# Values' products stored in two unsummed halves for ten of seventeen row tiles, and GpSimd's rotation issued behind VectorE's scalings

## The chip, the cores and the metric

The kernel runs on one core of one Trainium2 chip. Its five engines are TensorE (PE in the profile; PEld are its weight loads), VectorE (DVE), ScalarE (ACT), GpSimd (POOL) and SyncE (SP), which issues the DMAs. Each engine works through its own queue in order and waits there for what other engines and DMAs have to deliver. The metric is the device time of one execution in microseconds (us).

## The reference

One layer of a hybrid decoder: sliding-window attention (A) and gated linear attention (B) side by side, one output projection over both, then a squared-ReLU MLP, for 2048 prompt positions and 8 x 8 sample positions, with D = 1024. Cut to what the change touches (normalisations, the branch B and the MLP are left out):

```python
q = rope(q); k = rope(k)                       # 8 query heads, 2 key heads, 64 wide
s = einsum(q, k) * 64**-0.5                    # 128 queries against 256 keys, banded
m = maximum(max(s), sink)
p = exp(s - m);  p = p / (sum(p) + exp(sink - m))
attn = einsum(p, v)                            # 512 columns
mix = concat([attn, gla_out]) @ w_out          # 512 + 512 columns -> 1024
x = x + rms_norm(mix)
```

## The kernel before, in words

**Stages.** The rows are cut in 16 tiles of 128 prompt rows and one of 64 sample rows (NTILE = 17, NB = 16). Attention runs from about 30 to 305 us of the profiled span, the gated linear attention to about 735, the output projection to about 911, the MLP to the end.

**Precision.** Float32 products are made of parts: an operand is copied to a rounded high half by ScalarE, and VectorE forms the low half as the difference (`split_copy`, L226, does both: ScalarE in L228, VectorE in L229). A product takes high by high, high by low and low by high.

**Attention.** The loop `for i in range(NB)` (L794) takes a row tile in an iteration, with four `unit`s (L458), each for one key head r and two of its query heads (jj). A unit goes: scores (PE, tile `sc`), mask and maximum (DVE, a custom instruction that writes `s` and `m`), exponential (ACT, with the sum into `den`), reciprocal of `den` and two scalings of `s` by it (DVE, TENSOR_SCALAR), transposes `pT` (PE), the halves `ph` (ACT) and `pl` (DVE), the product `av` (PE). The values `vv` hold high and low half side by side, 64 columns each, so that `av` has two halves of 64 partitions, which must be summed: ACT copies the upper half to `rest`, and DVE adds it to the lower one into `mo` (64 partitions x 256). When the four units of a tile are done, one DMA stores `mo` to DRAM (`mix_d`), through `stores` and `store` (L326).

Three units are under way at a time (`behind`, `now`, `ahead`). What belongs to coming tiles is put between them: the table `A_PLAN` (L58) says at which unit (0 to 3) and which phase (A, X, B, C) the step `do` (L821) issues a piece: `x_norm` (L316, name "junk"), the projections' results (`take_first`, `take_rest`, L350 and L356), the halves of x (`x0`, `x1`), the low halves of queries and keys (`lo0`, `lo1`) and the rotation ("turn", `rotate`, L378). Between them PE gets projection matmuls (`proj`) as filling (`A_FILL`). The wrappers `te`, `ac` and `dv` hold the order of the program on PE, ACT and DVE (all under the line of the helper, L141). GpSimd and SyncE have no such wrapper: a scheduler places their instructions by what is ready.

**GpSimd in an iteration:** the rotation of a coming tile (two products `tb` with the sines, L385; the product `qk` with the cosines, L391; two sums into `rot`, L394 and L400), casts that copy keys to the other 64 partitions (L432 to L443), the sinks' columns of `s` (L466), and in eight of the iterations two subtractions for the weights of the next stage (`split_gw`, L273).

**Output projection.** `load_mix` (L1299) loads a tile's 1024 columns with one DMA (L1311) and splits them; `out_projecting` (L1324) makes two halves of 512 output columns with 24 matmuls each, over k = 0 to 7 blocks of 128 mix columns (L1337; 0 to 3 are attention's, 4 to 7 the other branch's). `residual` (L1507) normalises, adds and prepares the MLP's input; its powers run on GpSimd (L218). The order of the tiles is 0, 4, 1, 5, 2, 6, 3, 7, sample, 8, 12, 9, 13, 10, 14, 11, 15.

Of the kernel before, what the change touches and what calls it, by code (L numbers as in the profile page):

```python
# [21 lines left out]
P = 128  # L22
# [35 lines left out]
A_PLAN = [(name, (int(at[0]), at[1])) for name, at in dict(  # L58
    first="1B", hi1="3B", x1="1B", lo1="0A", x0="0C", rest="3A", lo0="3A", junk="2A", turn="1A", rstd="1A", vl="3B"
).items()]  # L60
G_FIRST = (0, 1)
G_NEXT = (NB, *range(2, NB))
G_ORDER = (3, 0, 1, 2)
G_FILL, G_GM = (38, 14, 13), 9
G_LAST = 32
G_HELD = 5
S_WAIT = (2, 3, 6)
WO_PARTS = ((), (0, 1, 2), (3, 4, 5), (6, 7))
# [58 lines left out]
def f32(ap):  # L127
    return ap.bitcast(F32)
# [23 lines left out]
def hybrid_step_kernel(ctx: ExitStack, tc: tile.TileContext, I, O):  # L152
# [12 lines left out]
    def rows(i):  # L165
        return min(P, NTOK - i * P)
# [25 lines left out]
    dpool = ctx.enter_context(tc.tile_pool(name="dpool", bufs=1, space=DRAM))  # L192
    mix_d = [dpool.tile([P, KT, rows(i)], F32, name=f"mix_d{i}") for i in range(NTILE)]
    xt_d = [dpool.tile([P, 2, KT, rows(i)], F32, name=f"xt_d{i}") for i in range(NTILE)]
    h_d = [dpool.tile([P, 7, KT // 2, BT], F32, name=f"h_d{sb}") for sb in range(NSB)]
# [90 lines left out]
    gxTs, ropes, xs_in, xTs, proj, qks, rots, heads, vals = {}, {}, {}, {}, {}, {}, {}, {}, {}  # L286
    stores = []

# [37 lines left out]
    def store():  # L326

        for dst, src in stores:
            nc.sync.dma_start(dst, src)
        stores.clear()  # L330

    def project(i, c, kind="a", wide=0):
# [23 lines left out]
    def take_rest(i):  # L356

        n = rows(i)
        p_ = proj.pop((i, 1))
        w = 640 - A_N  # L360
        scaled(qks[i].rearrange("p h d -> p (h d)")[:n, A_N:640], i, p_[:n, :w])
        vps = p_[:n, w:A_N]
        if i == NB:
            vals[i] = vn = sp.tile([NS, P], F32, tag="vv", name="vn", bufs=4)
            scaled(vn, i, vps)
            return lambda: None
        vals[i] = vv = sp.tile([P, 2, 2, HD], F32R, tag="vv", name=f"vv_{i}", bufs=4)
        vh, vl = vv[:, :, 0, :], vv[:, :, 1, :]
        vps = vps.rearrange("p (r d) -> p r d", r=2)
        scaled(vh, i, vps)  # L370
        if i == NB - 1:
            vo = sp.tile([P, P], F32, tag="kc", name="vo", bufs=1)
            scaled(vo, i, p_[:n, w:A_N])
            stores.append((O["v_win_prompt"][0, 0].rearrange("w h d -> w (h d)"), vo))
        rs = rstd_all[:n, i : i + 1]
        return lambda: dv.scalar_tensor_tensor(vl, vps, rs, f32(vh), op0=ALU.mult, op1=ALU.subtract)

    def rotate(i, engine=nc.gpsimd):  # L378
# [78 lines left out]

    def unit(i, r, jj, mo):  # L458

# [30 lines left out]
        for u in range(2):  # L490
            dv.tensor_scalar(s[:, u, :nk], s[:, u, :nk], den[:, u : u + 1], None, op0=ALU.mult)
        yield
        pT = bank([P, nkt, 2, P], "c", f"pT_{u_}")
# [14 lines left out]
        both = [v.rearrange("p u d -> p (u d)") for v in both]  # L508
        out = mo[rr, jj * 2 : jj * 2 + 2].rearrange("p j q -> p (j q)")
        if nkt == 1:  # L510
            te.matmul(av[:HD], hi[0], ph[:, 0], start=True, stop=False)
            te.matmul(av[:HD], hi[0], pl[:, 0], start=False, stop=False)
            te.matmul(av[:HD], lo[0], ph[:, 0], start=False, stop=True)
            yield
            ac.activation(out, av[:HD], AF.Copy)
        else:
            te.matmul(av, both[0], ph[:, 0], start=True, stop=False)
            for kt in range(2):
                te.matmul(av[:HD], hi[kt], pl[:, kt], start=False, stop=False)
            te.matmul(av, both[1], ph[:, 1], start=False, stop=True)  # L520
            yield
            rest = sp.tile([P, 2 * P], F32, tag="spc", name=f"rest_{u_}", bufs=2)
            ac.activation(rest[:HD], av[HD:], AF.Copy)
            yield
            dv.tensor_tensor(out, av[:HD], rest[:HD], op=ALU.add)
        if (r, jj) == (1, 1):
            stores.append((mix_d[i][:, 0:4, :], mo))
        yield

    def sample_unit(c, r, cached, kcs, mo):  # L530
# [39 lines left out]
        yield  # L570
        pc = sp.tile([P, 2, P], F32, tag="spc", name=f"spc_{r}_{c}", bufs=2)
        dv.tensor_copy(pc[:, 0, :], pt[:, 0, :])
# [206 lines left out]
    def units():  # L779
        for i in range(NB):  # L780
            mo = sp.tile([P, 4, P], F32, tag="mo", name=f"mo_{i}", bufs=2)
            for u in range(4):
                yield unit(i, u // 2, u % 2, mo)
# [10 lines left out]
    for i in range(NB):  # L794
# [18 lines left out]
        new = i + 3 < NTILE  # L813
        todo["turn"] = lambda: run(rotate(i + 1))
        if i + 2 < NTILE:
            todo["first"] = lambda: take_first(i + 2)
            todo["rest"] = lambda: todo.update(vl=take_rest(i + 2))
        if new:
# [6 lines left out]

        for u in range(4):
            for unit_ in (behind, now) if u in A_PL_FIRST else (now, behind):
                next(unit_, None)
# [33 lines left out]
    fill = chain(fill, *(projecting(t, gxTs[t], G_LATE, ac) for t in G_FIRST))  # L862
    for n in range(4):
        later = next(queue, None)
        next(now)
# [426 lines left out]
    def first_mixes():  # L1292
        ln, lh = logs[NB - 1]
        for i in B_ORDER[:2]:
            with tc.issue_after(ln.ins), tc.issue_after(lh.ins):
                deque(load_mix(i), 0)
            yield

    def load_mix(i, lo=None, hi=None):  # L1299
        n = rows(i)  # L1300
# [9 lines left out]
        ks = KT // 2 if i == NB - 1 else KT  # L1310
        nc.sync.dma_start(f32(m[:, 0, :ks, :n]), mix_d[i][:, :ks])  # L1311
        yield
        if i == NB:
            split_copy(m[:, 1, :, :NS], m[:, 1, :, NS:], f32(m[:, 0, :, :NS]))
            mixes[i] = m[:, 1], None
            return
        split_copy(m[:, 1, :ks, :n], m[:, 2, :ks, :n], f32(m[:, 0, :ks, :n]))
        parts = [[m[:, u, k, :n] for k in range(ks)] for u in (1, 2)]
# [5 lines left out]
    def out_projecting(te, i, banks, kinds="aabb"):  # L1324
# [3 lines left out]
        for c in range(2):  # L1328
            p_ = next_bank(kinds, f"out_{i}_{c}")
            cc = slice(c * 512, (c + 1) * 512)  # L1330
            for k in range(KT):
                if i == NB:
                    products = [(mh[:, k], w) for w in wo[k]]
                else:
                    products = (mh[k], wo[k][0]), (mh[k], wo[k][1]), (ml[k], wo[k][0])
                for u, (x, w) in enumerate(products):
                    te.matmul(p_, x, w[:, cc], start=k + u == 0, stop=k == KT - 1 and u == len(products) - 1)  # L1337
                    yield
            banks.append(p_)
# [96 lines left out]
    turned, logs, seconds = {}, {}, []  # L1436
    early = []
    fill = products()
# [35 lines left out]
    for p in H_EARLY:  # L1474
        h_place(0, p)
    U, R = {}, {}
    open_pools(U, ("raw", "xs", "ah", "al", "bh", "bl", "st1", "t"), "u")
# [753 lines left out]
```

## Time and profile before

| what | value |
|---|---|
| median of three runs | 2219.06 us (2218.36 to 2219.94) |
| the profiled execution's own time | 2217.48 us |
| its span, first to last instruction | 2215.7 us |
| ACT busy in the span | 1222.5 us (55%) |
| POOL busy in the span | 250.6 us (11%) |
| PE's granted clock, mean of the span | 0.999 |

The profiler's times are counted from the span's first instruction; 1.8 us of the execution lie outside it. A line of a timeline is: start in us, duration in us, engine, source line, operation, output<-input by the program's names, and the shape; "x2" are two instructions shown as one, and a bracket at the end tells how long the engine sat idle before it and what ended that. A group line holds a count, then the least, median and greatest duration in ns, and the first and last start. A window's line holds its bounds and length, then the busy time of PE, PEld, DVE, ACT and POOL, the mean granted clock, the DMA share and GB/s.

### The profile page before, as it was taken

How to read it: one execution, taken by the hardware profiler on the slowest of the kernel's cores; microseconds unless marked ns; L12 is line 12 of the kernel's file. 1: busy time of each engine (PE TensorE's matmuls, PEld its weight loads, DVE VectorE, ACT ScalarE, POOL GpSimd, SP SyncE). 2: the span in 40 equal slices, each digit the busy share in tenths (PEclk: the TensorE clock that was granted, in tenths of full speed). 3: DMA queues.
4: the chain of work that ended last, by engine and by line, in shares of the span. 5: the costliest groups of instructions: out<-in, count | busy, mean ns of one | idle time of the engine just before them, and what ended most of it. 6: DMA issues, size and time to landing. Idle time of an engine off the chain costs nothing.

```text
span 2215.7 us, 34304 instructions
## 1 busy us (share of the span) xinstructions
PE 2177.0 (98%) x11947; PEld 1865.5 (84%) x11947; DVE 1580.2 (71%) x3221; ACT 1222.5 (55%) x2549; POOL 250.6 (11%) x408
## 2 busy tenths in 40 slices
PE   8999999999999999999999999999999999999998
PEld 8888888899999888888888888888888888888886
DVE  5888877777778776687667788878545545855557
ACT  6777766555566443555555655555444444554445
POOL 3466522111111110000000000000000000000000
PEclk9999999999999999999999999999999999999999
DMA  7343322121113455765555766766765755866665
GB/s 240 120 139 138 108 95 89 57 73 62 53 49 120 157 192 195 261 224 185 200 189 189 273 208 212 242 233 221 230 207 178 232 175 184 292 232 217 219 196 202
DMA packets 229798, 392.64 MB, mean 177 GB/s; under 512 B 23379, under 2 KB 137882, under 8 KB 225642
## 3 DMA queue, kind: packets, MB, share of 16 engines
q1 hardware_dynamic: 229626, 390.47, 52.3%
q8 instruction: 94, 1.54, 0.3%
q14 instruction: 78, 0.64, 0.1%
HBM read 255.54 MB, written 135.86 MB: 177 GB/s over the span
## 4 chain that ended last, share of the span: by engine, by line
PE 83%; DVE 10%; ACT 5%; issue 2%; DMA 1%; POOL 0%; SPq 0%; DVEq 0%; ACTq 0%; POOLq 0%
PE dn L141 27%; PE gproj L141 10%; PE uc L141 7%; PE ua L141 7%; PE out L1337 6%; PE ud L141 4%; PE ub L141 4%; PE ue L141 4%; DVE s L141 2%; PE out L141 2%; PE sam L141 1%; PE proj L141 1%; PE gm L141 1%; PE dsam L141 1%; DVE pl L141 1%
## 5 line engine op out<-in xcount | busy, mean ns | idle before, releaser
L141 PE MATMUL dn<-ot,os 128*128 128x512 f32 x2688 | 621.2, 389 | 0.6 <-DVE ot L141 0.4
L141 PEld LDWEIGHTS dn<-ot,os 128*128 128x128 f32 x2688 | 504.2, 188 | 107.1 <-DVE ot L141 2.0
L141 DVE TENSOR_TENSOR os<-os 128x512 fp32r<-128x512 f32 x224 | 154.7, 690 | 228.1 <-ACT os L141 228.0
L141 ACT ACTIVATE os<-os 128x512 fp32r<-128x512 f32 x224 | 141.4, 631 | 278.1 <-DMA os<-s_d 219.5
L141 PE MATMUL gproj<-wg,gx 128*128 128x384 f32 (+1 forms) x1408 | 269.0, 343 | 0.0
L141 PEld LDWEIGHTS gproj<-wg,gx 128*128 128x128 f32 x1408 | 244.1, 188 | 5.0 <-issue 3.3
L141 ACT ACTIVATE st<-st 128x512 f32<-128x512 f32 x225 | 142.3, 633 | 137.4 <-DVE st L141 132.2
L141 PE MATMUL ua<-H,w 128*128 128x512 f32 x744 | 179.7, 390 | 0.3 <-DVE w L141 0.3
L141 PE MATMUL uc<-H,s 128*128 128x512 f32 x744 | 179.0, 389 | 0.0
L141 PEld LDWEIGHTS uc<-H,s 128*128 128x128 f32 x744 | 139.4, 188 | 29.2 <-DVE st L141 0.4
L141 PEld LDWEIGHTS ua<-H,w 128*128 128x128 f32 x744 | 138.5, 188 | 29.2 <-DVE w L141 1.1
L218 POOL TENSOR_TENSOR frs<-rs_v,half 128x1 f32<-128x1 f32 (+1 forms) x13 | 9.8, 751 | 1222.6 <-DVE rs_v L141 1222.6
L141 DVE TENSOR_TENSOR st<-st 128x512 f32<-128x512 f32 x160 | 110.4, 692 | 48.6 <-ACT st L141 45.4
L1337 PE MATMUL out<-wo,mt 128*128 128x512 f32 x608 | 141.5, 391 | 0.0
L1337 PEld LDWEIGHTS out<-wo,mt 128*128 128x128 f32 x608 | 113.2, 188 | 23.0
L141 ACT ACTIVATE s<-t 128x1024 fp32r<-128x1024 f32 x62 | 65.7, 1059 | 62.7 <-PE ue L141 24.6
L141 DVE TENSOR_TENSOR s<-t,s 128x1024 fp32r<-128x1024 f32 x62 | 75.9, 1225 | 33.9 <-ACT s L141 31.0
L141 DVE TENSOR_TENSOR ot<-ot 128x512 fp32r<-128x512 f32 x128 | 88.2, 689 | 10.9 <-ACT ot L141 9.8
L141 PE MATMUL proj<-wa_hi,xh 128*128 128x384 f32 (+1 forms) x272 | 95.2, 353 | 0.9 <-ACT wa_hi L141 0.6
L141 PE MATMUL proj<-wa_lo,xh 128*128 128x384 f32 (+1 forms) x272 | 93.9, 349 | 0.0
L141 PE MATMUL proj<-wa_hi,xl 128*128 128x384 f32 (+1 forms) x272 | 92.7, 345 | 0.0
L141 ACT ACTIVATE ot<-ot 128x512 fp32r<-128x512 f32 x128 | 80.8, 631 | 17.5 <-DMA ot<-t_d 13.5
(424 smaller groups left out, 4053.2 us busy)
## 6 DMA issues: line engine op xcount, KB each, us to landing
os<-s_d SPq DMA_DIRECT2D x224, 256.0 KB, 2.8
s_d<-st SPq DMA_DIRECT2D x31, 1792.0 KB, 8.9
raw<-in_w_up SPq DMA_DIRECT2D x64, 512.0 KB, 6.8
ot<-t_d SPq DMA_DIRECT2D x128, 256.0 KB, 3.2
rt<-in_w_down SPq DMA_DIRECT2D x96, 256.0 KB, 3.0
t<-in_w_down SPq DMA_DIRECT2D x64, 256.0 KB, 3.3
t_d<-t SPq DMA_DIRECT2D x32, 512.0 KB, 7.0
gx<-xt_d SPq DMA_DIRECT2D x28, 512.0 KB, 5.3
```

The lines of the kernel that those rows point to most:

```text
L141: ins = call(*a, **k)
L218: nc.gpsimd.tensor_tensor(out, v[:n], e, op=ALU.pow)
L1337: te.matmul(p_, x, w[:, cc], start=k + u == 0, stop=k == KT - 1 and u == len(products) - 1)
```

## The change

**1. Sums left out in ten tiles.** `FOLDED` names the tiles that keep the sum (0, 1, 4, 11, 14, 15, 16). In the others ACT copies all 128 partitions of `av` to a tile of its own (`mq`), and DVE adds nothing; the halves go to DRAM apart, the lower to `mix_d`, the upper to a new `low_d`. Stores are now issued unit by unit at the start of the next one (`store_folds`), 64 x 256 each: 4 for a tile that keeps its sum, 8 for one that doesn't, 104 for the 16 prompt tiles in place of 16.

**2. The sum is made later.** `load_mix` loads `low_d` too, into a single buffer `low` (the first, of tile 5, into another place), GpSimd adds the attention half of the loaded tile to it (128 x 512), and the split runs in two halves of 512 columns, the other branch's first.

**3. The order of k.** The output projection takes the blocks 4 to 7 first, then 0 to 3.

**4. The rotation.** That of tile i+2 is issued in iteration i at 3C (`tb`, `tb`, `qk`) and in iteration i+1 at 0C (`rot`, `rot`), each behind a GpSimd memset of the `den` of the unit scaled last, which has to wait for VectorE's scalings. Tile 1's stays as it was.

```diff
+    first="1B", ..., turn="1A", rstd="1A", vl="3B", begin="3C", turned="0C"
+K_ORDER = (4, 5, 6, 7, 0, 1, 2, 3)
+FOLDED = (0, 1, 4, 11, 14, 15, 16)
...
+    def store_folds():
+        for dst, src in folds:
+            nc.sync.dma_start(dst, src)
+        folds.clear()
...
+    def behind_scaling():
+        if not scaled_by:
+            return nullcontext()
+        return tc.issue_after(nc.gpsimd.memset(scaled_by[-1], 0.0).ins)
...
         for u in range(2):
             dv.tensor_scalar(s[:, u, :nk], s[:, u, :nk], den[:, u : u + 1], None, op0=ALU.mult)
+        scaled_by.append(den)
...
-            rest = sp.tile([P, 2 * P], F32, tag="spc", name=f"rest_{u_}", bufs=2)
-            ac.activation(rest[:HD], av[HD:], AF.Copy)
-            yield
-            dv.tensor_tensor(out, av[:HD], rest[:HD], op=ALU.add)
-        if (r, jj) == (1, 1):
-            stores.append((mix_d[i][:, 0:4, :], mo))
+            if i in FOLDED:
+                rest = sp.tile([P, 2 * P], F32, tag="spc", name=f"rest_{u_}", bufs=1)
+                ac.activation(rest[:HD], av[HD:], AF.Copy)
+                yield
+                dv.tensor_tensor(out[:HD].rearrange("p j q -> p (j q)"), av[:HD], rest[:HD], op=ALU.add)
+            else:
+                ac.activation(out.rearrange("p j q -> p (j q)"), av, AF.Copy)
+                yield
+        for half, to in zip(half_of, (mix_d, low_d)):
+            if to is mix_d or i not in FOLDED:
+                folds.append((to[i][rr, jj * 2 : jj * 2 + 2, :], out[half]))
...
-        todo["turn"] = lambda: run(rotate(i + 1))
+        if i == 0:
+            todo["turn"] = lambda: run(rotate(1))
+        def begin_turn(turn):
+            with behind_scaling():
+                run(turn, 2)
+            todo["turned"] = lambda: end_turn(turn)
+        def end_turn(turn):
+            with behind_scaling():
+                run(turn)
...
+            todo["begin"] = lambda: begin_turn(rotate(i + 2))
...
+        if i not in FOLDED:
+            low = fold_place()
+            nc.sync.dma_start(low, low_d[i])
...
+            nc.gpsimd.tensor_tensor(low, low, raw[:, :4], op=ALU.add)
+            split_copy(m[:, 1, 4:], m[:, 2, 4:], raw[:, 4:])
+            split_copy(m[:, 1, :4], m[:, 2, :4], low)
```

**Three places in the order of instructions.** The first is GpSimd's queue between iterations 6 and 7, where tile 8 is rotated; `kl` are the keys' casts, `s` the sinks' columns, `wg` the weights of the next stage. Before:

```order
L443 CAST kl_7_2230<-kl_7_2230 64x128
L385 TENSOR_TENSOR tb_8_2393<-qk_8_2182,rope_8_1506 128x10x32 x2
L391 TENSOR_TENSOR qk_8_2182<-qk_8_2182,rope_8_1506 128x640
L394 TENSOR_TENSOR rot_8_2397<-qk_8_2182,tb_8_2393 128x2x4x64
L400 TENSOR_TENSOR rot_8_2397<-qk_8_2182,tb_8_2393 128x128
L466 COPY s_7_1_0_2327<-sink_401 128x2
L443 CAST kl_7_2230<-kl_7_2230 64x128
L437 CAST kl_8_2492<-kl_7_2230 128x2x128
L466 COPY s_7_1_1_2403<-sink_401 128x2
L273 TENSOR_TENSOR wg3_1_190<-wg3_raw6_2116,wg3_0_189 128x400
```

and with the change:

```order
L458 CAST kl_7_2282<-kl_7_2282 64x128
L391 MEMSET den_6_1_1_2312 128x2
L400 TENSOR_TENSOR tb_8_2363<-qk_8_2233,rope_8_1547 128x10x32 x2
L406 TENSOR_TENSOR qk_8_2233<-qk_8_2233,rope_8_1547 128x640
L481 COPY s_7_1_0_2385<-sink_417 128x2
L458 CAST kl_7_2282<-kl_7_2282 64x128
L452 CAST kl_8_2548<-kl_7_2282 128x2x128
L391 MEMSET den_7_0_0_2379 128x2
L409 TENSOR_TENSOR rot_8_2444<-qk_8_2233,tb_8_2363 128x2x4x64
L415 TENSOR_TENSOR rot_8_2444<-qk_8_2233,tb_8_2363 128x128
L481 COPY s_7_1_1_2459<-sink_417 128x2
L276 TENSOR_TENSOR wg3_1_206<-wg3_raw6_2169,wg3_0_205 128x400
```

The products now stand behind a memset of unit (6,1,1)'s sums, and the sums `rot` have moved behind the casts and behind a second memset, of unit (7,0,0)'s.

The second is VectorE's queue at the scalings of unit (7,1,1), a tile that no longer sums; `vv` are values, the ISA rows the masks of the next unit. Before:

```order
L141 RECIPROCAL den_7_1_1_2521<-den_7_1_1_2521 128x2
L141 TENSOR_SCALAR s_7_1_1_2403<-s_7_1_1_2403,den_7_1_1_2521 128x256 x2
L141 TENSOR_TENSOR mo_7_2199<-av_7_1_0_2544,rest_7_1_0_2549 64x256
L141 SCALAR_TENSOR_TENSOR vv_9_2525<-proj_9_1_2339,rstd_all_175,vv_9_2525 128x2x64
L855 COPY c_864_1520<-c_raw1_1512 64x8
L141 ISA s_8_0_0_2462,m_8_0_0_2579<-sc_8_0_0_2556,amask_206,sink_401 128x256
```

and with the change:

```order
L143 RECIPROCAL den_7_1_1_2578<-den_7_1_1_2578 128x2
L143 TENSOR_SCALAR s_7_1_1_2459<-s_7_1_1_2459,den_7_1_1_2578 128x256 x2
L143 SCALAR_TENSOR_TENSOR vv_9_2582<-proj_9_1_2397,rstd_all_191,vv_9_2582 128x2x64
L889 COPY c_864_1560<-c_raw1_1552 64x8
L143 ISA s_8_0_0_2518,m_8_0_0_2641<-sc_8_0_0_2612,amask_222,sink_417 128x256
```

The sum `mo` is gone; everything else stands as it stood.

The third is GpSimd's queue in the output projection, where before there are only the powers of `residual`; with the change:

```order
L221 TENSOR_TENSOR ssq1_199<-rs_v_9661,half_189 128x1
L1364 TENSOR_TENSOR mo0_5048<-mo0_5048,mt_5_9664 128x512
L1364 TENSOR_TENSOR low_9897<-low_9897,mt_2_9895 128x512
L221 TENSOR_TENSOR ssq0_198<-rs_v_9798,half_189 128x1
L221 TENSOR_TENSOR ssq1_199<-rs_v_9874,half_189 128x1
L221 TENSOR_TENSOR ssq0_198<-rs_v_9960,half_189 128x1
L1364 TENSOR_TENSOR low_9991<-low_9991,mt_6_9989 128x512
```

The late sums (L1364) of tiles 5, 2 and 6 stand among the powers, those of tiles 5 and 2 ahead of a power of tile 0.

More of the change, by code (lines that the diff above doesn't have):

```diff
@@ L58 @@
 A_PLAN = [(name, (int(at[0]), at[1])) for name, at in dict(
-    first="1B", hi1="3B", x1="1B", lo1="0A", x0="0C", rest="3A", lo0="3A", junk="2A", turn="1A", rstd="1A", vl="3B"
+    first="1B", hi1="3B", x1="1B", lo1="0A", x0="0C", rest="3A", lo0="3A", junk="2A", turn="1A", rstd="1A", vl="3B", begin="3C", turned="0C"
 ).items()]
 G_FIRST = (0, 1)
+K_ORDER = (4, 5, 6, 7, 0, 1, 2, 3)
 G_NEXT = (NB, *range(2, NB))
@@ L193, in hybrid_step_kernel @@
     mix_d = [dpool.tile([P, KT, rows(i)], F32, name=f"mix_d{i}") for i in range(NTILE)]
+    low_d = [dpool.tile([P, 4, P], F32, name=f"low_d{i}") for i in range(NB)]
     xt_d = [dpool.tile([P, 2, KT, rows(i)], F32, name=f"xt_d{i}") for i in range(NTILE)]
@@ L286, in hybrid_step_kernel @@
     gxTs, ropes, xs_in, xTs, proj, qks, rots, heads, vals = {}, {}, {}, {}, {}, {}, {}, {}, {}
-    stores = []
+    stores, folds, scaled_by = [], [], []
     stages = [("cache_k", 1), ("cache_v", 1), ("s", 3), ("ph", 2), ("pl", 2), ("qh", 2), ("ql", 2), ("mo", 2), ("tb", 1)]
@@ L456, in heads_T, with unit @@
         }
-    def unit(i, r, jj, mo):
+    def unit(i, r, jj):
         nkt = min(i + 1, 2)
@@ L508, in unit @@
         both = [v.rearrange("p u d -> p (u d)") for v in both]
-        out = mo[rr, jj * 2 : jj * 2 + 2].rearrange("p j q -> p (j q)")
+        out = sp.tile([P, 2, P], F32, tag="mq", name=f"mq_{u_}", bufs=4)
         if nkt == 1:
+            assert i in FOLDED
             te.matmul(av[:HD], hi[0], ph[:, 0], start=True, stop=False)
@@ L514, in unit @@
             yield
-            ac.activation(out, av[:HD], AF.Copy)
+            ac.activation(out[:HD].rearrange("p j q -> p (j q)"), av[:HD], AF.Copy)
         else:
@@ L570, in sample_unit @@
         yield
-        pc = sp.tile([P, 2, P], F32, tag="spc", name=f"spc_{r}_{c}", bufs=2)
+        pc = sp.tile([P, 2, P], F32, tag="mq", name=f"spc_{r}_{c}", bufs=4)
         dv.tensor_copy(pc[:, 0, :], pt[:, 0, :])
@@ L780, in units @@
         for i in range(NB):
-            mo = sp.tile([P, 4, P], F32, tag="mo", name=f"mo_{i}", bufs=2)
             for u in range(4):
-                yield unit(i, u // 2, u % 2, mo)
+                yield unit(i, u // 2, u % 2)
         mo = sp.tile([P, 4, NS], F32, tag="mo", name="mo_s", bufs=2)
@@ L826, in hybrid_step_kernel @@
         for u in range(4):
+            store_folds()
             for unit_ in (behind, now) if u in A_PL_FIRST else (now, behind):
@@ L863, in hybrid_step_kernel @@
     for n in range(4):
+        store_folds()
         later = next(queue, None)
@@ L1297, in first_mixes, with fold_place @@
             yield
+    def fold_place():
+        if not R:
+            return next(mos)
+        return R["x"].tile([P, 4, P], F32, tag="low", name="low", bufs=1)
     def load_mix(i, lo=None, hi=None):
@@ L1316, in load_mix @@
             return
-        split_copy(m[:, 1, :ks, :n], m[:, 2, :ks, :n], f32(m[:, 0, :ks, :n]))
+        raw = f32(m[:, 0])
+        if i in FOLDED:
+            split_copy(m[:, 1, :ks, :n], m[:, 2, :ks, :n], raw[:, :ks, :n])
+        else:
+            nc.gpsimd.tensor_tensor(low, low, raw[:, :4], op=ALU.add)
+            split_copy(m[:, 1, 4:], m[:, 2, 4:], raw[:, 4:])
+            split_copy(m[:, 1, :4], m[:, 2, :4], low)
         parts = [[m[:, u, k, :n] for k in range(ks)] for u in (1, 2)]
@@ L1330, in out_projecting @@
             cc = slice(c * 512, (c + 1) * 512)
-            for k in range(KT):
+            for n, k in enumerate(K_ORDER):
                 if i == NB:
@@ L1336, in out_projecting @@
                 for u, (x, w) in enumerate(products):
-                    te.matmul(p_, x, w[:, cc], start=k + u == 0, stop=k == KT - 1 and u == len(products) - 1)
+                    te.matmul(p_, x, w[:, cc], start=n + u == 0, stop=n == KT - 1 and u == len(products) - 1)
                     yield
@@ L1436, in hybrid_step_kernel @@
     turned, logs, seconds = {}, {}, []
-    early = []
+    early, R = [], {}
     fill = products()
@@ L1475, in hybrid_step_kernel @@
         h_place(0, p)
-    U, R = {}, {}
+    U = {}
     open_pools(U, ("raw", "xs", "ah", "al", "bh", "bl", "st1", "t"), "u")
```

## The prediction

> **What bounds the kernel now.** I begin with the engines' shares and the busy time by stage, then take the waits of PE in the attention, since the change lies mostly there, and last the chain of waits through one iteration. The first line is the page's, the next two are windows of the attention and of the output projection (PE, PEld, DVE, ACT, POOL), the last two PE's longest waits in the first window.
>
> ```profile
> PE 2177.0 (98%) x11947; PEld 1865.5 (84%) x11947; DVE 1580.2 (71%) x3221; ACT 1222.5 (55%) x2549; POOL 250.6 (11%) x408
> 60.00:290.00 230.00, 214.94 (x1419) 195.72 (x1417) 201.35 (x580) 173.84 (x471) 133.72 (x238) 1.00 0.36 124
> 740.00:905.00 165.00, 165.00 (x792) 137.46 (x791) 110.95 (x173) 72.55 (x152) 19.29 (x31) 1.00 0.62 209
> PE pT L141 <- DVE s L141: 6.7, 15, 0.5
> PE sc L141 <- DVE qh L141: 1.8, 10, 0.2
> ```
>
> Over the whole span PE is the bound, and in the output projection it never sits idle (165.00 of 165.00 us): there the change can only lose. In the attention PE shows 15.06 us of gaps and DVE is nearly as full; the longest wait is PE's transposes `pT` for DVE's scalings `s`, 15 times, once per iteration. An iteration lasts 17.47 us, from one `junk` square of ACT to the next:
>
> ```profile
> 202.60 1.04 ACT L141 ACTIVATE junk<-x 128x1024 bf16<-128x1024 f32 x1
> 220.07 1.04 ACT L141 ACTIVATE junk<-x 128x1024 bf16<-128x1024 f32 x1
> ```
>
> So PE's gaps are 15.06 / (230 / 17.47) = 1.14 us per iteration. The chain of waits through iteration 9 (start, duration, what) shows who sets its length:
>
> ```profile
> 205.23 0.61 ACT ph L141
> 205.87 0.69 DVE pl L141
> ...
> 207.70 1.51 DVE s L141 x2
> 209.24 0.42 DVE mo L141
> ...
> 211.80 0.69 DVE ql L141
> ...
> 213.62 0.42 DVE mo L141
> 214.06 0.69 DVE xl L141
> ...
> 215.57 0.60 DVE pl L141
> 216.24 0.55 PE av L141 x3
> ```
>
> From 205.87 to 216.24 the chain stays on DVE; before and after that stretch it is on ACT and PE. What shortens DVE's queue within it shortens the iteration, as long as PE keeps up.
>
> **The rotation.** The scalings at 207.70 take 1.51 us for the two. Their group, then the same pair later in the iteration, and what POOL does beside the three:
>
> ```profile
> L141 DVE TENSOR_SCALAR s<-s,den x106: 344/354/958, 60.1 to 289.6; 128x256 f32<-128x256 f32 x106
> 212.73 0.86 DVE L141 TENSOR_SCALAR s<-s,den 128x256 f32<-128x256 f32 x2
> 216.59 0.62 DVE L141 TENSOR_SCALAR s<-s,den 128x256 f32<-128x256 f32 x2
> 207.32 1.74 POOL L385 TENSOR_TENSOR tb<-qk,rope 128x320 f32<-128x320 f32 x2 [0.15 <-ACT qk L141]
> 213.04 0.40 POOL L437 CAST kl<-kl 128x256 fp32r<-128x256 f32 x1
> ```
>
> One scaling has a median of 0.354 us, and an undisturbed pair takes 0.62. Beside `tb` (POOL until 209.06) the second scaling ends at 209.21: DVE is held until POOL's instruction is over. The casts hold the second pair the same way, for 0.24 us. So a POOL instruction that runs across a scaling blocks it. With `tb` issued behind the scalings the pair takes 0.62 in place of 1.51: **-0.89 us**. What follows:
>
> ```profile
> 209.86 0.60 ACT L141 ACTIVATE ph<-pT 128x512 fp32r<-128x512 f32 x1 [1.41 <-PE pT L141]
> 210.76 0.68 DVE L141 TENSOR_TENSOR pl<-pT,ph 128x512 fp32r<-128x512 f32 x1
> 213.24 0.60 ACT L141 ACTIVATE xh<-xT 128x512 fp32r<-128x512 f32 x1 [0.61 <-PE xT L141]
> 212.55 0.66 PE L141 MATMUL xT<-ident,x 128*128 128x128 f32 x4
> 216.22 0.45 PE L141 MATMUL av<-pl,vv 128*64 128x256 f32 x2 [0.20 <-DVE rs_v L141]
> ```
>
> `pl` (210.76) and `ql` (211.80) move by 0.89. `xT` starts 0.06 after `ql` ends, so it and `xh` move along; `xl`, now at 214.06, may start as soon as `xh` ends (213.84), 0.2 us sooner still. That makes 1.08 us by the time PE takes `av`<-`pl` (216.22), where it waited 0.20 for DVE. The rest of the iteration is ACT's and PE's and stays. Fifteen rotations are moved: 15 x 1.08 = **-16.2 us**. That is next to all of PE's gaps (1.14 per iteration), but a gap shows only what the pipelined records leave open, so I take it as reachable.
>
> **The sums left out.** Sixty `mo` sums of 0.416 us:
>
> ```profile
> L141 DVE TENSOR_TENSOR mo<-av,rest x60: 416/417/419, 56.9 to 315.1; 64x256 f32<-64x256 f32 x60
> L141 ACT ACTIVATE rest<-av x60: 380/381/383, 56.5 to 314.5; 64x256 f32<-64x256 f32 x60
> ```
>
> Forty of them go, 40 x 0.45 with the step between instructions = 18 us of DVE. Little of it is on the path. The first of an iteration (209.24) lies ahead of `pl`, which without it waits for `ph` (scalings end 208.32, `pT`, `ph` 208.97 to 209.57): `pl` gains 1.18 in place of 0.89, 0.29 more. The second lies ahead of `xl`, which waits for `xh` by then. And `xT` can follow `ql` only as far as PE's own matmuls let it, and PE is busy for 93% of the window, so of the 0.29 I take half, 0.15 x 10 = **-1.5 us** (bounds 0 and -2.9). ACT's copy of 128 instead of 64 partitions stays at 0.381: each partition's row is as long as before. The stores are more, 104 for 16:
>
> ```profile
> L329 SPq DMA_DIRECT2D mix_d<-mo x16: 319/327/1209, 61.8 to 315.6; - x16
> ```
>
> 88 x 0.33 = 29 us of SP's issuing over 260 us. SP works ahead of the loads it issues (x four tiles early); its cover is this lead, and if it went, each iteration's loads would come 1.9 us later. I cost it at nothing.
>
> **What the moved rotation meets.** `tb` now starts behind the scaling that ends at E, and the rest of POOL's queue is pushed behind it:
>
> ```profile
> 212.44 0.19 POOL L466 COPY s<-sink 128x2 f32<-128x2 f32 x1
> 209.13 1.57 POOL L391 TENSOR_TENSOR qk<-qk,rope 128x640 f32<-128x640 f32 x1
> 210.78 1.29 POOL L394 TENSOR_TENSOR rot<-qk,tb 128x512 f32<-128x512 f32 x1
> 214.41 1.99 POOL L273 TENSOR_TENSOR wg<-wg_raw,wg 128x384 fp32r<-128x384 f32 x2
> L273 POOL TENSOR_TENSOR wg<-wg_raw,wg x16: 1010/1029/1055, 106.8 to 232.9; 128x400 fp32r<-128x400 f32 x8, 128x384 fp32r<-128x384 f32 x8
> ```
>
> The trace has no such memset; I price it as the copy of 128x2, 0.19 us, and with it `tb` (1.74) and `qk` (1.57) occupy POOL until about E + 3.7. The next pair, 212.73 before with E at 209.21, starts near E + 3.2 (3.52 less the 0.29 of a sum left out): held for up to 0.5, mostly under the wait for `xh`. I take **+2 us** for the fifteen (0 to 15 x 0.5 = 7). `rot` stands behind that pair's memset, ends near E + 6.6 and pushes the two `wg` subtractions, 1.99 us, to E + 6.7 to 8.7. The third pair (216.59, so E + 7.4, less the same 0.29 and the 0.2 of `xl`: E + 6.9) meets them and would end at E + 8.9 in place of E + 7.5, 1.4 late; PE has other work ahead of that pair's `pT`, for which I credit half, so 0.7 in each of the eight iterations that have them: **+5.8 us** (0 to 11). `heads_T`, which needs `rot`, follows the `junk` square at 220.07; with E at 208.3 `rot` ends near 214.9 and is early.
>
> **The output projection.** Each of ten tiles adds on POOL one 128x512 sum (1.29, by `rot`), and splits in two halves. A tile's matmuls, the split ahead of it and the loads:
>
> ```profile
> 819.50 3.89 PE L1337 MATMUL out<-wo,mt 128*128 128x512 f32 x16
> 818.05 1.23 DVE L229 TENSOR_TENSOR mt<-mt 128x1024 fp32r<-128x1024 f32 x1 [0.93 <-ACT mt L228]
> mt<-mix_d SPq DMA_DIRECT2D x14, 512.0 KB, 4.6
> os<-s_d SPq DMA_DIRECT2D x224, 256.0 KB, 2.8
> 722.11 1.38 DVE L1049 TENSOR_TENSOR after<-after,before 128x128 f32<-128x128 f32 x1
> 721.94 1.40 POOL L990 TENSOR_TENSOR sg<-sg,gp 128x512 f32<-128x512 f32 x1 [3.44 <-ACT sg L989]
> ```
>
> The split of this tile ended 0.22 us ahead of PE. With the other branch's half first, that half is ready sooner (half of 1.23), and the attention half has 12 matmuls more, 12 x 3.89 / 16 = 2.9 us. It needs POOL's sum, ACT's copy (as `xh`) and DVE's difference (as `xl`), 1.3 + 0.6 + 0.7 = 2.6 us, all behind the later of two loads; the second, of 256 KB, is issued a step of 0.33 behind the first and by the page's other loads of its size takes 2.8 us against 4.6, so it is no later. I take **+0.5 us** (0 to 2), mostly for tile 0, whose powers now stand behind two sums.
>
> The Trainium skill, "SBUF — State Buffer", section "SBUF: two separate sides", speaks against this part: it says VectorE and GpSimd share a port pair as an exclusive lock, which a VectorE instruction with two SBUF inputs can lose too, for a whole GpSimd instruction. The two rows at 722 us agree: DVE's `after` takes 1.38 us beside POOL's sum. By the rule each of the ten late sums holds one DVE instruction for up to 1.3 us, which would be +13 us if all of it reached PE.
>
> The sum: -16.2 - 1.5 + 2 + 5.8 + 0.5 = -9.4. The profiled execution took 2217.48 us (span 2215.7), 1.6 below the median 2219.06, to which the result will be compared. So 2219.06 - 9.4 = 2209.7; I say **2209**.
>
> **The rivals.**
> (a) *Nothing is hit anew:* the products, the sums and the `wg` subtractions fall between the scalings, and DVE's queue gains all, 16.2 to 19: 2200 to 2203. For it: POOL is busy for 133.72 of 230 us only. Against: those are 10.2 us in each 17.47, in pieces of up to 2 us, and the order puts them one behind the other.
>
> (b) *PE is the bound anyway:* it wins only the 6.7 us of its waits for `s` and the 1.5, and the new collisions cost 6 to 8 of that: 2217 to 2219, no change. For it: PE is busy for 93% of the window. Against: the waits behind `qh` and `rs_v` are DVE's as well and shrink too.
>
> (c) *Slower: the output projection stalls on the late half.* If the second load shares the DMA queues with the first and lands 1 us behind it, and a DVE difference is held once by a POOL sum (1.3 us), the chain is 2.6 + 1.0 + 1.3 = 4.9 us against the 2.9 of cover: PE stalls 2 us a tile. On eight tiles that is 16 us against a gain of 9.4: 2219 + 6.6, or 2226. It decides from 9.4 / 8 = 1.2 us a tile. For it: one buffer, one queue in order, and no slack in that stage. Against: a tile lasts 48 x 3.89 / 16 = 11.7 us and its load 4.6, so there is time to issue early.
>
> (d) *The memset doesn't order POOL behind both scalings.* The order rows show it ahead of `tb`, and `den` is read by both scalings, so it stays within (b).
>
> **How the numbers follow.** My forecast, 2204 to 2214: 0.47. (a) 0.17. (b), with collisions that eat the gain, 2215 to 2223: 0.22. (c) 0.14. About 0.2% (4.4 us) is what a measurement of this kernel can tell from no change; faster means below 2214.6, slower above 2223.5. That gives faster 0.64, same 0.22, slower 0.14. The range 2199 to 2221 holds the forecast, (a), most of (b) and little of (c).
>
> **What would show it.** The scalings' maximum of 958 ns falls or moves to pairs beside `wg` and `qk`; PE's wait `pT` <- `s` (6.7) shrinks; the iteration, 17.47, falls to about 16.4 without `wg` and 17.1 with it; `mo` counts 20; the whole gain is there when the attention ends (near 305), and windows of the output projection stay at PE 165 of 165. It is wrong if the iteration shortens and the output projection gives it back as waits of PE for `mt`, or if PE's waits move to another producer and the iteration keeps its length.

## The result, and the profile after

The changed kernel takes 2204.87 us (median of four runs, 2204.45 to 2205.03) against 2218.85 us before (four runs; 2219.06 was the median of the first three): 14.0 us less, a ratio of 0.9935 with a 95% interval of 0.9922 to 0.9947. The prediction said 2209, most likely 2204 to 2214, within 2199 to 2221. The profiled executions differ by 13.0 us (spans of 2215.7 and 2202.7).

The page's first line, the two windows and PE's waits in the attention, as they were read before (in the windows' rows: bounds, length, then busy time of PE, PEld, DVE, ACT and POOL):

```profile
PE 2173.4 (99%) x11947; PEld 1866.8 (85%) x11947; DVE 1565.2 (71%) x3191; ACT 1219.6 (55%) x2559; POOL 267.1 (12%) x448
60.00:290.00 230.00, 227.09 (x1530) 212.35 (x1529) 196.54 (x586) 183.05 (x511) 143.34 (x278) 1.00 0.46 143
740.00:905.00 165.00, 161.24 (x774) 133.77 (x773) 111.98 (x171) 72.08 (x152) 28.98 (x37) 1.00 0.66 215
PE pT L143 <- DVE s L143: 1.3, 6, 0.3
PE sc L143 <- DVE qh L143: 0.6, 3, 0.2
```

PE's gaps in the first window fell from 15.06 to 2.91 us, and its wait for the scalings from 6.7 to 1.3 us. (The window now takes in 20 us of the next stage; from 60 to 265 us, within the attention alone, the gaps are 2.56 us in 205.) In the output projection, where PE had no gap, it now has 3.76 us of them. So there are two movements of opposite sign. Where the stages begin tells their size. The rows are the first matmuls of the next stage (`gproj`), which PE reaches when the attention's own work allows it, the first and last of the output projection, and the first of the MLP, all with count, least, median and greatest duration, and first and last start; before, then after:

```profile
L141 PE MATMUL gproj<-wg,gxh x128: 331/338/449, 288.8 to 343.5; 128*128 128x384 f32 x96, 128*128 128x400 f32 x32
L141 PE MATMUL out<-wo,mt x120: 387/389/498, 711.2 to 908.1; 128*128 128x512 f32 x120
L141 PE MATMUL ua<-H,s24h x8: 389/389/498, 927.9 to 930.3; 128*128 128x512 f32 x8
```

```profile
L143 PE MATMUL gproj<-wg,gxh x128: 335/338/449, 269.8 to 324.0; 128*128 128x384 f32 x96, 128*128 128x400 f32 x32
L143 PE MATMUL out<-wo,mt x120: 387/389/507, 693.2 to 894.4; 128*128 128x512 f32 x120
L143 PE MATMUL ua<-H,s24h x8: 389/389/497, 914.3 to 916.7; 128*128 128x512 f32 x8
```

The attention is over 288.8 - 269.8 = **19.0 us** earlier. The output projection, from its first matmul to the MLP's, went from 216.7 to 221.1 us: **4.4 us** back. The stages between and after it are 1.6 us longer together (422.4 to 423.4, and 1287.8 to 1288.4). That is the 13.0. For the 1.0 us PE's clock is enough: in the changed kernel's profile its mean is 0.55 from 368 to 370 us and 0.59 from 370 to 372, which loses (0.45 + 0.41) x 2 = 1.7 us, and before it stays at full speed through that stage. Over all the kernels below, that stage lasts 421.6 to 422.4 us without such a fall, 423.2 to 423.8 with one, and 425.2 with two.

The iteration shortened from 17.47 to 16.42 us where GpSimd also subtracts for the weights:

```profile
190.01 1.05 ACT L143 ACTIVATE junk<-x 128x1024 bf16<-128x1024 f32 x1
206.40 1.05 ACT L143 ACTIVATE junk<-x 128x1024 bf16<-128x1024 f32 x1
222.82 1.05 ACT L143 ACTIVATE junk<-x 128x1024 bf16<-128x1024 f32 x1
```

Within it, the timeline shows the first scalings free, and the weights' subtractions (`wg`) across the third:

```profile
194.85 0.62 DVE L143 TENSOR_SCALAR s<-s,den 128x256 f32<-128x256 f32 x2
195.61 0.10 POOL L391 MEMSET den<- 128x2 f32 x1 [1.29 <-ACT ql L143]
195.67 1.71 POOL L400 TENSOR_TENSOR tb<-qk,rope 128x320 f32<-128x320 f32 x2
197.46 1.56 POOL L406 TENSOR_TENSOR qk<-qk,rope 128x640 f32<-128x640 f32 x1
198.73 0.71 DVE L143 TENSOR_SCALAR s<-s,den 128x256 f32<-128x256 f32 x2
201.84 2.02 POOL L276 TENSOR_TENSOR wg<-wg_raw,wg 128x384 fp32r<-128x384 f32 x2
202.39 1.63 DVE L143 TENSOR_SCALAR s<-s,den 128x256 f32<-128x256 f32 x2
```

The pair beside `tb`, 1.51 us before, takes 0.62; the second pair 0.71 (0.86 before); the third 1.63 (0.62 before), because it now meets `wg`. The memset takes 0.10 us.

In the output projection PE's longest waits are these, and one late sum of GpSimd with what VectorE and ScalarE do beside it:

```profile
PE xnT L1608 <- ACT ht L1616: 2.8, 1, 2.8
PE out L1386 <- DVE mt L232: 1.0, 2, 0.5
```

```profile
835.08 1.29 POOL L1364 TENSOR_TENSOR low<-low,mt 128x512 f32<-128x512 f32 x1 [1.82 <-DMA mt<-mix_d]
835.67 1.25 DVE L232 TENSOR_TENSOR mt<-mt 128x512 fp32r<-128x512 f32 x1 [0.97 <-ACT mt L231]
836.40 0.63 ACT L231 ACTIVATE mt<-low 128x512 fp32r<-128x512 f32 x1 [0.77 <-POOL low L1364]
837.07 0.69 DVE L232 TENSOR_TENSOR mt<-low,mt 128x512 fp32r<-128x512 f32 x1
```

The same subtraction (128x512) takes 0.69 us alone and 1.25 beside the sum; it ends 0.55 us after the sum does. Seven of the ten sums hold a VectorE instruction in this way, for 0.5 to 1.1 us over what it takes alone, 5.4 us in all. Of the two waits of 0.5 us for a split the first follows a subtraction held for 0.5 us (at 801.04, 1.20 us in place of 0.69), the second a load for which ScalarE waited 5.2 us.

The wait of 2.8 us comes at the stage's end, for the last transposes, where PE has no further tile to work on in the meantime. The view names ScalarE's `ht`, but VectorE's normalisation `x`, which these transposes read, ended only 0.11 us before it, and it hangs on a load: `x` stands in VectorE's queue behind the split of the last tile, VectorE sat idle 2.69 us for that split's high half, and ScalarE 4.89 us until the tile's load had landed. So VectorE is not behind with work there; the load came late. It stands in SyncE's queue behind a load of `bx`, which waits for VectorE's `x` of an earlier tile. In this way a delay can pass from tile to tile; that is read from these rows, and no run tests it.

### The profile page after: what moved, and what is told of

The parts are those of the page before. It is cut to its first block, busy times and chain, and to the rows that moved or that the text cites. A ratio compares the mean times of both kernels' runs of the same rounds, so it can differ in the third digit from the quotient of the medians.

```text
span 2202.7 us, 34467 instructions
## 1 busy us (share of the span) xinstructions
PE 2173.4 (99%) x11947; PEld 1866.8 (85%) x11947; DVE 1565.2 (71%) x3191; ACT 1219.6 (55%) x2559; POOL 267.1 (12%) x448
## 4 chain that ended last, share of the span: by engine, by line
PE 55%; DVE 1%; ACT 0%; issue 0%; DMA 0%; DVEq 0%; ACTq 0%
PE dn L143 27%; PE ua L143 7%; PE uc L143 7%; PE ue L143 4%; PE ud L143 4%; PE ub L143 4%; PE sam L143 1%; PE dsam L143 1%; DVE st L143 0%; DMA os<-s_d 0%; ACT st L143 0%; DVE s L143 0%; DVE t L143 0%; DVE lfg L143 0%; DVE w L143 0%
## 5 line engine op out<-in xcount | busy, mean ns | idle before, releaser
L143 DVE TENSOR_TENSOR os<-os 128x512 fp32r<-128x512 f32 x224 | 154.8, 691 | 220.7 <-ACT os L143 220.1
```

Source lines behind the costliest of these rows:

```text
L143: ins = call(*a, **k)
```

## The experiments

Each kernel has its own profile. The table gives the median, the start of the next stage's projections (the attention's end), and the output projection's length as above, all in us. Runs 1 to 4, 5 to 8, 9 to 11 and 12 were each measured on one chip together with the kernel before, whose medians there are 2218.87, 2220.51, 2219.36 and 2218.40; the ratios are to these.

| kernel | median | ratio, 95% interval | attention ends | output projection |
|---|---|---|---|---|
| before | 2218.85 | | 288.8 | 216.7 |
| the change | 2204.87 | 0.9935 (0.9922 to 0.9947) | 269.8 | 221.1 |
| 1 rotation alone | 2205.97 | 0.9937 (0.9922 to 0.9952) | 274.2 | 217.8 |
| 2 unsummed alone | 2220.05 | 1.0003 (0.9993 to 1.0012) | 283.2 | 223.2 |
| 3 one wait of two | 2207.50 | 0.9944 (0.9927 to 0.9961) | 269.7 | 224.2 |
| 4 old order of k | 2205.49 | 0.9934 (0.9919 to 0.9949) | 269.8 | 222.4 |
| 5 weights behind scalings | 2205.17 | 0.9925 (0.9910 to 0.9940) | 268.5 | 221.6 |
| 6 three more summed | 2204.69 | 0.9927 (0.9912 to 0.9942) | 271.1 | 221.3 |
| 7 no late sum | 2199.77 | 0.9905 (0.9891 to 0.9920) | 269.7 | 216.6 |
| 8 no second load | 2210.71 | 0.9957 (0.9940 to 0.9973) | 270.1 | 227.2 |
| 9 sum on VectorE | 2203.67 | 0.9931 (0.9919 to 0.9944) | 270.1 | 219.6 |
| 10 = 9 and 5 | 2203.82 | 0.9925 (0.9913 to 0.9938) | 269.2 | 219.8 |
| 11 = 10, twelve tiles | 2203.05 | 0.9929 (0.9915 to 0.9942) | 268.5 | 220.7 |
| 12 = 10, five tiles | 2204.34 | 0.9939 (0.9926 to 0.9953) | 270.2 | 222.2 |

The attention's end repeats within 0.4 us where the attention is the same (the change, 4, 7, 8, 9: 269.8, 269.8, 269.7, 270.1, 270.1). The output projection does not: the same code for it gave 221.1 and 224.2 in the change and in run 3. PE's clock accounts for a good half of that. In run 3 PE waits 3.9 us at the stage's end, and then the clock falls (the mean granted clock is the number after the five engines' times):

```profile
888.00:890.00 2.00, 0.07 (x1) 0.10 (x2) 1.28 (x1) 0.66 (x2) 0.46 (x1) 1.00 1.06 268
890.00:892.00 2.00, 2.00 (x9) 1.95 (x10) 0.37 (x1) 0.74 (x2) 0.00 (x0) 0.50 0.88 324
892.00:894.00 2.00, 2.00 (x7) 1.58 (x6) 1.84 (x5) 1.61 (x5) 0.00 (x0) 0.65 0.08 33
```

That loses (0.50 + 0.35) x 2 = 1.7 us, and the wait is 1.1 us longer than the change's. Runs 2, 4 and 12 have one such fall in the output projection and run 8 has two, each about 1.7 us by the same sum and each within 1.5 us of the end of a wait of PE of 1.7 to 3.9 us; the other kernels have none there, though some waited as long (run 11 3.5 us). Less 1.7 us for each, the lengths are 221.5 (run 2), 222.5 (3), 220.7 (4), 223.8 (8) and 220.5 (12). Differences of 1 to 2 us there still say little by themselves.

**1. The rotation alone.**

```diff
-FOLDED = (0, 1, 4, 11, 14, 15, 16)
+FOLDED = tuple(range(NTILE))
```

> The moved rotation alone: every tile keeps its sum of the values' product, so that the output projection loads and splits as before. By the prediction's terms (16.2 us won, 7.8 lost to new collisions) about 2218.9 - 8.4 = 2210. By what the two traces show (the attention ends 19 us earlier, the output projection gives back 4.5) the new collisions cost little and nothing is given back: 2201 to 2204, faster than the whole change. If the sums left out carry the gain, 2213 or more.

Measured: 2205.97. The attention won 14.6 us, not 8.4, and the output projection lost 1.1, too little to tell. So the rotation carries nearly all of the gain, and the new collisions cost less than the prediction's 7.8. The chain of waits through one iteration of this run (start, duration, what) shows what they do cost:

```profile
182.57 0.10 POOL den L391
182.66 1.68 POOL tb L400 x2
184.41 0.37 POOL qk L406
...
187.04 1.25 POOL rot L409
188.30 0.43 POOL rot L415
188.72 0.13 POOL s L481
188.85 1.98 POOL wg L276 x2
190.84 0.56 POOL rstd_all L221
191.43 0.59 ACT qk L143
```

The chain, on VectorE before, is now on GpSimd: `rot` pushes the weights' subtractions back, these push the power `rstd_all`, and ScalarE's `qk` of the next tile waits for it. An ordinary iteration lasts 16.68 us with the subtractions and 16.13 without: 0.55 in each of eight. What the run does not separate: the rotation is both issued earlier in the program and made to wait for the scalings, and no run has the one without the other. The rows show only that the collision with `tb` is gone.

**2. The unsummed halves alone.**

```diff
-        if i == 0:
-            todo["turn"] = lambda: run(rotate(1))
+        todo["turn"] = lambda: run(rotate(i + 1))
...
-            todo["begin"] = lambda: begin_turn(rotate(i + 2))
```

> The unsummed halves alone, with GpSimd's rotation in its old place. By the prediction's terms 1.5 us won and 0.5 lost: 2218, and PE's wait for the scalings stays at 6.7 us. By what the two traces show the output projection loses 4.5, so 2219 to 2222. If the sums left out carry the gain, 2210 or less.

Measured: 2220.05, the same as before within the interval. The scalings are held as they were (the greatest is 957 ns, 958 before), the attention wins 5.6 us all the same, and the output projection loses 6.5. The two parts' gains in the attention, 14.6 and 5.6, add up to 20.2, near the 19.0 of both: the sums are worth 4.4 on top of the rotation.

**3. One wait of the two.**

```diff
         def end_turn(turn):
-            with behind_scaling():
-                run(turn)
+            run(turn)
```

> The whole change without the second wait: the sums of the rotation no longer stand behind a memset and follow the cosine product as soon as GpSimd's order lets them. If each wait is needed because a GpSimd instruction that runs across a scaling holds it until its own end, the second scalings of an iteration are held by the sums (1.3 us) and most of 15 x 1 us comes back: 2212 to 2219. If only the first collision cost time, 2204 to 2206, or less, since the weights' subtractions are no longer pushed onto the third scalings.

Measured: 2207.5, with runs from 2204.2 to 2210.6. The attention ends where it did with both waits, so the second wait does nothing for it, and my reason for it falls: the sums do not come between the scalings and hold them. In GpSimd's order `rot` stands there behind the sinks' copy, and it meets the second scalings from the other side:

```profile
198.55 0.71 DVE L143 TENSOR_SCALAR s<-s,den 128x256 f32<-128x256 f32 x2
198.79 0.25 POOL L481 COPY s<-sink 128x2 f32<-128x2 f32 x1
199.00 1.40 POOL L409 TENSOR_TENSOR rot<-qk,tb 128x512 f32<-128x512 f32 x1
```

The scalings began first and kept their 0.71 us; GpSimd's sum took 1.40 in place of 1.29. The time above the whole change's lies in the output projection (224.2), whose code is the same: by the rows above it comes from a longer wait at that stage's end and from PE's clock, and is not a result of the memset.

**4. The old order of k.**

```diff
-K_ORDER = (4, 5, 6, 7, 0, 1, 2, 3)
+K_ORDER = (0, 1, 2, 3, 4, 5, 6, 7)
```

> The whole change with the blocks of the output projection in their old order (attention's half first). If the late half is covered by the 12 matmuls of the other half, as the prediction has it, the ten tiles now stall for up to 2.6 us each: 2215 to 2230. If the loads come early enough anyway, the time stays at 2205.

Measured: 2205.49, no difference that can be told. The 2.9 us of cover, on which the prediction let the late half hang, are not needed: one wait of PE for a split (1.8 us, once) is all that its profile shows for it, and there ScalarE had itself waited 6.1 us for the tile's load.

**5. The weights' subtractions behind the third scalings.** They are collected and issued at unit 1, phase C, behind a memset as the rotation is.

```diff
-        nc.gpsimd.tensor_tensor(lo, raw, f32(hi), op=ALU.subtract)
+        los.append(lambda: nc.gpsimd.tensor_tensor(lo, raw, f32(hi), op=ALU.subtract))
...
+    def late_los():
+        if los:
+            with behind_scaling():
+                for late_lo in los:
+                    late_lo()
+            los.clear()
...
             do(u, "C")
+            if u:
+                late_los()
```

> The whole change, and GpSimd's two subtractions for the next stage's weights, which now run across the third scalings, are issued behind a memset of their sums too. By the prediction's price (0.7 us in each of eight iterations) 5.8 us less than the whole change's 2205: 2199. By the periods of the changed kernel (16.4 to 16.7 us with these subtractions, 15.9 to 16.2 without) 0.45 in each, so 2201. If the scalings aren't what limits these iterations, 2205.

Measured: 2205.17 (2200.95 to 2205.81). The collision went, the greatest scaling fell to 736 ns, and four of the eight iterations shortened from 16.4 to 15.9 us, but four others lengthened, by 0.2 to 0.4 us (16.68 to 17.09 in one). The subtractions had found other victims there: in each of the four VectorE converts a constant or a mask, and the conversion, 0.19 to 0.27 us in the change, now runs beside `wg` and takes 0.94 to 1.09. The attention won 1.3 us in all, not 3.6. The time didn't move beyond its interval. The run takes two things away at once, the collision with the third scalings and the subtractions' place ahead of the power `rstd_all`, so it doesn't tell which of them had cost the 0.55.

**6. Three more tiles that keep their sum.**

```diff
-FOLDED = (0, 1, 4, 11, 14, 15, 16)
+FOLDED = (0, 1, 4, 9, 10, 11, 13, 14, 15, 16)
```

> The whole change with three more tiles that keep their sum: 9, 10 and 13, the last ones that were unsummed in the order of the output projection. The attention loses about 3 x 0.45 = 1.4 us. If the output projection loses its 3 to 6 us because VectorE falls behind over the last tiles, and one wait of PE for a transposed result shows it at the end (2.8 us), that wait goes: 2202 to 2204 and a stage of 218. If it is lost elsewhere, 2206.

Measured: 2204.69, stage 221.3, with PE's wait at the end still 2.0 us. The last tiles are not where it is lost.

**7. No late sum.** The attention's columns of the ten tiles are made of the upper halves alone.

```diff
-            nc.gpsimd.tensor_tensor(low, low, raw[:, :4], op=ALU.add)
```

> The whole change without GpSimd's late sums: both loads and the two-part split stay, the stored lower halves are left out of the attention's columns. If the sums lock VectorE or lengthen the chain from load to split, and that is what the output projection pays, its stage falls from 221 to 218 and the time to 2201 to 2202. If the second load is what it pays, the time stays at 2205.

Measured: 2199.77, 5.4 us less than run 5 on the same chip, with a ratio whose interval lies below the change's, and the output projection back at 216.6. PE's window from 735 to 895 us is full in this run, and has 3.76 us of gaps in the change (first this run, then the change):

```profile
735.00:895.00 160.00, 160.00 (x767) 133.26 (x766) 109.06 (x175) 73.05 (x155) 18.45 (x30) 1.00 0.67 217
```

```profile
735.00:895.00 160.00, 156.24 (x747) 129.20 (x746) 111.33 (x172) 70.61 (x151) 29.73 (x38) 1.00 0.64 208
```

The second load and the split in two are still there, so neither is what the stage pays: it is GpSimd's sum. The loads fit a delay that is passed on to the end: both stages begin at 693 us, and the last tile's load is issued at 872.03 us in this run and at 876.47 in the change, 4.4 later.

Holding VectorE is one way in which the sum costs, and GpSimd's queue is another. In the change the sum at 765.00 us waits for its load with a power behind it, and VectorE sits idle 2.36 us for that power, where 0.73 is usual. In each kernel with GpSimd's late sums VectorE waits once to three times for a power for 1.5 to 4.1 us in this stage, and in the others never for more than 1.3. What each way costs is not separated.

**8. No second load.** The sum takes both operands from the first load.

```diff
-            nc.sync.dma_start(low, low_d[i])
...
-            nc.gpsimd.tensor_tensor(low, low, raw[:, :4], op=ALU.add)
+            nc.gpsimd.tensor_tensor(low, raw[:, :4], raw[:, 4:], op=ALU.add)
```

> The whole change without the second load: GpSimd's late sum takes both operands from the first load, so it still runs, but the stored upper halves are left out. If the second load (256 KB more, and a place in SyncE's queue behind the single buffer) is what the output projection pays, its stage falls from 221 to 218 and the time to 2201 to 2202. If the sum is, the time stays at 2205.

Measured: 2210.71, slower than the change, with a stage of 227.2. Without the load nothing is won, which agrees with run 7. Of the 6.1 us above the change's stage, 3.4 are PE's clock, which falls twice. For the rest the profile shows a wait of 2.0 us of PE at tile 8: the sum there, waiting for its load, kept a power behind it in GpSimd's queue, and VectorE's `x` waited 4.13 us for that power, with the next split behind it.

**9. The late sum on VectorE.**

```diff
-            nc.gpsimd.tensor_tensor(low, low, raw[:, :4], op=ALU.add)
+            nc.vector.tensor_tensor(low, low, raw[:, :4], op=ALU.add)
```

> The whole change with the late sum on VectorE in place of GpSimd, at the same place of the program. If GpSimd's sum costs the output projection its 4.5 us by holding VectorE, VectorE does the sum itself in about 0.69 us (a 128x512 difference of two SBUF operands) and is held no more: stage 216.6 to 219, time 2200 to 2203. If the later start of the split is what costs, or VectorE has no room for ten more instructions, 2205 or more.

Measured: 2203.67, stage 219.6. That is between the two: PE still waits 2.2 us at the end, for VectorE's `x`. VectorE is held no more but has ten instructions more (113.24 us busy in the window shown for run 7, where that run had 109.06). 219.6, and 219.8 in run 10, lie below the 220.7 to 223.8 of the kernels with ten sums on GpSimd, clock losses taken off, but by little more than the spread. So it is likely, and not shown, that the move takes away a part of the cost; the rest would be the ten instructions in VectorE's queue, since the stage without any late sum is 3 us shorter still.

**10, 11 and 12. Combinations.** 10 joins the edits of 9 and 5. 11 leaves tiles 11 and 14 unsummed too:

```diff
-FOLDED = (0, 1, 4, 11, 14, 15, 16)
+FOLDED = (0, 1, 4, 15, 16)
```

12 leaves only 2, 3, 5, 6 and 7 unsummed:

```diff
-FOLDED = (0, 1, 4, 11, 14, 15, 16)
+FOLDED = (0, 1, 4, *range(8, NTILE))
```

> The same with the weights' subtractions issued behind the third scalings as in the run before. If the two repairs add up: 1.3 to 3 us less than with the sum on VectorE alone, 2198 to 2201. If they don't, the same as that one.

> The same with tiles 11 and 14 unsummed as well (twelve of seventeen). If each unsummed tile is worth 0.45 us in the attention and the late sum on VectorE costs nothing in the output projection, 0.9 us less. If the two splits and the sum do cost PE there, the same or 1 us more.

> Only tiles 2, 3, 5, 6 and 7 unsummed (the ones whose sums fall into the longest iterations, and which come first in the output projection), the late sum on VectorE, the weights' subtractions behind the third scalings. Against the same with ten tiles (2203.8, profiled stage 219.8): the attention loses 5 x 0.27 = 1.4 us; if the output projection's loss is VectorE falling behind over consecutive unsummed tiles, it now has eleven tiles to catch up, PE's wait at the end goes and the stage falls to about 217.5, so 2202 to 2203. If that wait has nothing to do with the unsummed tiles before it, 2205.

Measured: 2203.82, 2203.05 and 2204.34. None is faster than the change by more than the intervals. Run 11 won 0.7 us in the attention over run 10 and gave 0.9 back in the output projection. Run 12 is inconclusive: PE's wait at the end fell to 0.8 us, as expected if the delay is caught up, but a wait of 1.7 us for a split came up at tile 8, which keeps its sum there, and PE's clock fell after it (another 1.7 us). That wait is the load's: ScalarE sat idle 6.34 us until the tile had landed. Its load stands in SyncE's queue behind the sample rows' `bx` and was issued at 796.75 us, 104.9 us into the stage, 1.9 later than in the change.

## Why the prediction was right, and where it was wrong

The direction, the mechanism of the first gain and the place of the loss were right, and the sum came near (-9.4 predicted, -14.0 measured) partly by luck: the gain in the attention was put 9.1 us too small and the loss in the output projection 3.9 too small, and these errors went against each other.

- **The held scalings: right.** `tb` running across a scaling held it; with `tb` behind it the pair takes the 0.62 us that the prediction gave it. "A POOL instruction that runs across a scaling blocks it" was too wide: the third pair in the prediction's rows takes its 0.62 us, and the trace has GpSimd's power `rstd_all` (128x1, at 216.35, 0.62 us) running across it. The gain per iteration was mis-sized: 1.08 us, while the undisturbed iteration of run 1 fell by 1.34 (17.47 to 16.13). The second pair is also held less there (0.86 to 0.71), which would make 0.15 of the 0.26; the rest was not traced.
- **New collisions: 7.8 us predicted, about 4.4 measured.** The +2 us for the cosine product did not come: it ends 0.3 us into the second pair, which is shorter than before. The +5.8 us for the weights' subtractions came as 8 x 0.55 = 4.4 us. The collision was at the predicted place, and longer (the third pair 1.63 us), but by run 1's chain the price is set by GpSimd's own queue, through the power behind the subtractions, of which the prediction said nothing. That is read from the chain; no run separates the two. Together the rotation was put at -8.4 and was -14.6.
- **The sums left out: -1.5 us predicted, -4.4 on top of the rotation and -5.6 alone.** In ordinary iterations each unsummed tile won 0.21 to 0.29 us (16.68 to 16.42 in one), about the 0.29 that was worked out and then halved for PE's sake; the halving was wrong. And three tiles, 5 to 7, won 1.06, 0.59 and 0.75: in their iterations VectorE also converts constants, and in run 1 `tb` held one conversion in each. With the sum gone, the conversion starts just ahead of `tb` and is not held. In the first of the three iterations, run 1 and then the change:

```profile
130.56 2.03 POOL L400 TENSOR_TENSOR tb<-qk,rope 128x320 f32<-128x320 f32 x2
130.80 1.05 DVE L889 CAST c<-c_raw 128x448 uint8<-128x448 f32 x1
```

```profile
129.50 0.38 DVE L889 CAST c<-c_raw 128x448 uint8<-128x448 f32 x1
129.59 1.86 POOL L400 TENSOR_TENSOR tb<-qk,rope 128x320 f32<-128x320 f32 x2
```

The three conversions take 1.05, 0.63 and 0.60 us in run 1 and 0.38, 0.18 and 0.15 in the change, 1.57 less together. Without them the three tiles won 0.39, 0.14 and 0.30, on average as much as the others. So some 1.6 of the 4.4 us are again a hold that went away, by the timing alone.

- **The output projection: +0.5 predicted (0 to 2), +4.4 measured.** This is the step that failed most. The prediction counted the late sum as a link between load and split, with 2.9 us of cover, and left its hold of VectorE to the sentence on the Trainium skill; the 0.5 us stood mostly for the powers of tile 0 behind two sums. Runs 4 and 7 show that the cover hardly matters and the sum is all of it, by its hold of VectorE and by the powers behind it, in shares that stay open. The Trainium skill's page, "SBUF — State Buffer", section "SBUF: two separate sides", was the better guide here: the lock it tells of agrees with the rows at 835 us, and of the 13 us that ten full holds would make, 5.4 were taken from VectorE; the stage grew by 4.4.
- **Rival (a), nothing is hit anew,** gave 16.2 to 19 us for the attention. The attention's 19.0 is that by chance, since the collisions did happen. **Rival (b), PE is the bound anyway,** fell: the attention shortened by 19.0 us, where PE's waits for the scalings were 6.7. **Rival (c)** had the right stage and half of the right cause (the held difference), but the late second load, its other half, is excluded by run 7, where that load is still there and PE has no gap; and it took 4.4 us, not 16.
- **The stores: no price seen.** Run 2 has all 104 of them and the attention still gains; no run varies them alone.

What stays open: how the cost of the late sum divides between the hold of VectorE and GpSimd's queue, the same question for the weights' subtractions, and why PE's clock falls after some of its waits and not after others as long.

## What to carry to other kernels

Where two engines hold each other, ask of each GpSimd instruction which VectorE instruction it runs across, and order the one behind the other before giving either less work: here moving the rotation was worth 14.6 us in its stage, and 18 us of VectorE's work left out was worth 4.4 on top. A sum that is put off to a stage in which PE never waits has to be priced there by what it holds up on the other engine and behind it in its own queue, and not only by its own chain. And a price from one iteration holds for iterations with the same neighbours: look for those that carry something else. An instruction that is moved out of one collision can meet another, as the weights' subtractions met the conversions in run 5.

## What the runs showed of the hardware that was not expected

The time for which an instruction of VectorE is held doesn't go by its own size. A sum of 128x1 from two SBUF operands, 0.15 us otherwise, took 1.25 us beside a GpSimd sum, and GpSimd's own sum was stretched when VectorE was there first (1.69 us in place of 1.29). Not every overlap holds: before the change, GpSimd's power of 128x1 ran across a pair of scalings in 12 iterations, and these pairs took 0.62 to 0.64 us. The rows of the sum:

```profile
819.82 2.08 DVE L1626 TENSOR_TENSOR ht<-ht 128x512 f32<-128x512 f32 x3
821.35 1.69 POOL L1364 TENSOR_TENSOR low<-low,mt 128x512 f32<-128x512 f32 x1 [2.77 <-DMA mt<-mix_d]
821.81 1.25 DVE L1425 TENSOR_TENSOR ssq<-ssq 128x1 f32<-128x1 f32 x1
```

A wait of PE can cost more than its own length: after some of them, of 1.7 to 3.9 us, the granted clock was at half for long enough to lose another 1.7 us.
